# Two GLU steps earlier, in other buffers, and some additions from POOL to DVE

## The chip, the cores and the metric

The kernel runs on one core of a Trainium2 chip. The metric is the device time of one execution in microseconds (us), as the median of several runs. Engines are named as in the profile: PE multiplies matrices (PEld is its loading of weights), DVE, ACT and POOL work elementwise, SP issues transfers.

## What is computed

One layer of a streaming encoder over 2048 tokens of width 1024, all in float32.

```
hn = rmsnorm(h);  u, g_ssm, q, k, v, g_attn = split(hn @ W_in)
y_ssm = GLU(GELU(S5(u)))  * silu(g_ssm)     # zz = z @ w_glu + b;  val * sigmoid(gate)
y_att = stick_breaking(q, k, v, 8 heads x 64) * silu(g_attn)
h = h + concat(y_ssm, y_att) @ W_out
out = h + sigmoid(rmsnorm(h) @ W_pg) * (p @ W_pp)
```

Stick-breaking attention is swept in 128-query blocks over all earlier keys: a sigmoid of the scores, a reversed running product along the keys, and a product with the values.

## The kernel before

float32 products are made of three matmuls each (a high and a low part of both sides: hi·hi, hi·lo, lo·hi). The program has four stages in time: the projection of `u` with the S5 preparation, the S5 batches, the attention, and the output products.

The attention is a loop over 40 steps `t`. The eight heads are four pairs `hp`; pair `hp` handles query block `i = t - 8*hp`, so two pairs are under way in most steps, in steps 30 and 31 pairs 2 (blocks 14 and 15) and 3 (blocks 6 and 7), and from step 32 on pair 3 alone. Two blocks ahead of its attention a block is projected (`attn_proj`: 48 matmuls into `ps_q` on two banks, three transposes into `ps_tq`). `attn_block` walks the keys in chunks of 512, last chunk first. One chunk is a *turn*: six matmuls into two score banks `ps_z` (one per head), a sigmoid on ACT (`px`, L816), the running product on DVE (a scan, L821, which also reads `ps_z`), transposes into `ps_wt` (L526), two copies on ACT (`ws`, L835), and matmuls with the values into `ps_o` (L843). In a block's first chunk POOL masks the diagonal (L819).

Which PSUM banks these take is set by the step: before `glu_at` scores have three banks (`z0`, `z1`, `tr`) and projections `acc` and `ssm`; from `glu_at` on scores have two banks and projections `acc` and `tr`, since the GLU takes `ssm` (gate half, `ps_g`) and `acc` (value half, `ps_v`).

`glu_at` is 32. From then on every step has two of the 16 GLU units. A unit reads a 512x512 tile of the GELU output (`glu_z` loads it as `zt` and splits it into `zr`, once for four units), makes 24 matmuls, a sigmoid on ACT (L696), a product on DVE (L76), a product with the loaded gate on POOL (L698), and a store. Its buffers `gsm` and `glus` have two copies each. Every step from 32 on also makes one set of `cross_sums`: four loads, four subtractions on POOL (L874 to L877) and four stores, which prepare weights for the output products (a Strassen-like scheme with seven products in place of eight).

Key and value tiles lie in numbered slots; slots 2, 5, 6 and 7 are in pool `kv2`. Slot 6 holds keys of pair 1 last, slots 2, 5 and 7 keys of pair 2, up to step 31. Pool `wx` holds the first four weight tiles of pair 2, which its projections read up to step 29. The GLU's pool opens at step 32, where `kv2` and `wx` were.

In the output stage `cross_products` runs for eight pairs of blocks in `mixed_pair` and eight in `gated_pair`: on POOL it makes four additions `sx` (L912) per pair, each then split for a product by ACT (`yr`, L513) and DVE (`yr`, L65). The gated pairs end with a product on DVE, an addition on POOL (L1026) and a store.

The order on each engine is not that of the source: `plan` collects what each instruction needs, and `arrange` sets one fixed order per engine from estimated durations. The engines then run through their rows in that order, each waiting where an operand is late.

Of the kernel before, what the change touches and what calls it, by code (L numbers as in the profile page):

```python
# [8 lines left out]
F32 = mybir.dt.float32  # L9
# [4 lines left out]
ALU = mybir.AluOpType  # L14
# [4 lines left out]
P = 128  # L19
SEQ = 2048  # L20
DM = 1024
NT = SEQ // P
# [4 lines left out]
L = 16  # L27
# [643 lines left out]
def glu_z(e, pool, tb):  # L671

    zf = e.z_d.rearrange("j (k p) c -> p k j c", p=P)
    zr = pool.tile([P, 2, 4, 512], F32R, tag="zr", name="zr", bufs=1)
    for k in range(4):
        n = NCH // 4
        zt = pool.tile([P, L, n], F32, tag="zt", name="zt", bufs=2)
        e.nc.sync.dma_start(zt, zf[:, k, :, tb * n:(tb + 1) * n])
        hi, lo = (zr[:, s, k].rearrange("p (c j) -> p c j", j=L) for s in range(2))
        split(e, hi, lo, zt.rearrange("p j c -> p c j"))  # L680
    return zr


def glu_unit(e, pool, w, zr, tb, m):
    nc = e.nc
    gt = pool.tile([P, 512], F32, tag="gsm", name="gsm", bufs=2)
    nc.sync.dma_start(gt, e.gs_d[tb][m * P:(m + 1) * P])
    pg = e.bank("ps_g2", "ssm")
    pv = e.bank("ps_v2", "acc")
    cs = slice(m * P, (m + 1) * P)  # L690
    for half, ps in ((1, pg), (0, pv)):
        for c in range(4):
            wt = w[half][c]
            mm3(e, ps, (wt[:, 0, cs], wt[:, 1, cs]), (zr[:, 0, c], zr[:, 1, c]), c == 0, c == 3)
    sg = pool.tile([P, 512], F32, tag="glus", name="glus", bufs=2)
    nc.scalar.activation(sg, pg, AF.Sigmoid, bias=e.bglu[:, 4 + m:5 + m])  # L696
    stt(nc, sg, pv, e.bglu[:, m:m + 1], sg, ALU.add, ALU.mult)
    nc.gpsimd.tensor_tensor(sg, sg, gt, op=ALU.mult)  # L698
    nc.sync.dma_start(e.ys_d[tb][m * P:(m + 1) * P], sg)
# [158 lines left out]
    A.w += load_w(e, [cols[c, :, :, P * A.hp:P * (A.hp + 1)] for c in range(lo, hi)], 512, e.gmix, at=lo, **kw)  # L858


def cross_sums(e, pool, src, dst, scale, c):

    nc = e.nc
    t = []
    for i, j in ((0, 0), (0, 1), (1, 1), (1, 0)):
        a = pool.tile([P, 512], F32, tag="cs", name="cs", bufs=4)
        k = 4 * i + c
        nc.sync.dma_start(a, src[k * P:(k + 1) * P, 512 * j:512 * j + 512])
        if scale is not None:
            nc.scalar.activation(a, a, AF.Copy, scale=scale[:, k:k + 1])  # L870
        t.append(a)
    b11, b12, b22, b21 = t
    gp = nc.gpsimd.tensor_tensor
    gp(b11, b12, b11, op=ALU.subtract)  # L874
    gp(b12, b22, b12, op=ALU.subtract)
    gp(b22, b22, b11, op=ALU.subtract)
    gp(b21, b21, b22, op=ALU.subtract)  # L877
    for k, a in enumerate((b11, b22, b12, b21)):
        nc.sync.dma_start(dst[k][c * P:(c + 1) * P], a)
# [20 lines left out]
    return load_w(e, [d[c * P:(c + 1) * P] for c in range(4)], 512, None, **kw)  # L900


def cross_products(e, pool, name, q, w, early, late):

    nc = e.nc

    def f(tag, n):
        return pool.tile([P, 512], F32, tag=tag, name=tag, bufs=n)

    def add(a, b, op=ALU.add):  # L910
        t = f("sx", 3)
        nc.gpsimd.tensor_tensor(t, a, b, op=op)  # L912
        return t

    def product(ps, a, k, first):
        y = pool.tile([P, 2, 4, P], F32R, tag="yr", name="yr", bufs=4)
        split(e, y[:, 0].rearrange("p c t -> p (c t)"), y[:, 1].rearrange("p c t -> p (c t)"), a)
        for c in range(4):
            mm3x(e, ps, (y[:, 0, c], y[:, 1, c]), (w[k][c][:, 0], w[k][c][:, 1]), first and c == 0, c == 3, not first)

    ps = [e.bank(name, "z0", "z1", "acc", "ssm", "w0", "w1") for _ in range(4)]
    product(ps[0], q[0], 0, True)
    s1 = add(q[2], q[3])
    s2 = add(s1, q[0], ALU.subtract)
# [12 lines left out]
    late(3, None, None)  # L937
    s4 = add(q[1], s2, ALU.subtract)
    product(ps[2], s4, 5, False)
    late(1, ps[2], u)  # L940
    product(ps[3], q[3], 6, False)
    late(2, ps[3], u)


def mixed_pair(e, pool, far, j):

    nc = e.nc
    dma = (nc.sync if j else nc.gpsimd).dma_start
    q, h = [], []
    for k in range(4):  # L950
        i = 2 * j + k // 2
        y = pool.tile([P, 512], F32, tag="yq", name="yq", bufs=5)
        v = y.rearrange("p (c t) -> p c t", c=4)
        if k % 2:
            dma(v, e.ya_d[i].rearrange("c p t -> p c t"))
        else:
            dma(v, e.ys_d[i // 4][:, (i % 4) * P:(i % 4 + 1) * P].rearrange("(c p) t -> p c t", p=P))
        q.append(y)
    for k in range(4):
        i = 2 * j + k // 2  # L960
        x = far.tile([P, 512], F32, tag="h", name="h", bufs=7)
        dma(x, e.x[0, i * P:(i + 1) * P, 512 * (k % 2):512 * (k % 2) + 512])
        h.append(x)
    ss = pool.tile([P, 2, 2], F32, tag=f"ss{j}", name="ss")

    def early(u, ps, n):
        if n == 0:
            for k in (3, 1, 2):
                nc.gpsimd.tensor_tensor(h[k], h[k], u, op=ALU.add)
        vt(nc, h[3], ps, h[3], ALU.add)  # L970

    def late(k, ps, u):
        if ps is not None:
            vt(nc, h[k], ps, h[k], ALU.add)
        i, m = k // 2, k % 2
        jk = far.tile([P, 512], F32, tag="sg", name="jk", bufs=4)
        nc.scalar.activation(jk, h[k], AF.Square, accum_out=ss[:, i, m:m + 1])
        nc.sync.dma_start(e.h_d[2 * j + i][:, 512 * m:512 * m + 512], h[k])

    cross_products(e, pool, "ps_h", q, e.wo, early, late)  # L980
    r = pool.tile([P, 2], F32, tag=f"rs{j}", name="rs")
    vt(nc, r, ss[:, :, 0], ss[:, :, 1], ALU.add)
    vs(nc, r, r, 1.0 / DM, ALU.mult, EPS, ALU.add)
    nc.gpsimd.tensor_tensor(r, r, e.mhalf[:, :2], op=ALU.pow)
    return r


def gated_pair(e, pool, far, j, rs):

    nc = e.nc  # L990
    q, h = [], []
    for k in range(4):
        i, m = k // 2, k % 2
        t = far.tile([P, 512], F32, tag="h", name="h", bufs=7)
# [12 lines left out]
    o = [None] * 4  # L1007
# [6 lines left out]
    def late(k, ps, u):  # L1014
        i, m = k // 2, k % 2
        if o[k] is None:
            o[k] = far.tile([P, 512], F32, tag="sg", name="sg", bufs=4)
            if u is not None:
                vt(nc, o[k], ps, u, ALU.add)
        nc.scalar.activation(o[k], ps if k == 0 else o[k], AF.Sigmoid, scale=rs[:, i:i + 1])  # L1020
        pp = e.bank("ps_p", "tr", "o")
        ts = slice(i * P, i * P + P)
        for c in range(2):
            mm3x(e, pp, (pr[:, 0, c, ts], pr[:, 1, c, ts]), (e.wp[m][c][:, 0], e.wp[m][c][:, 1]), c == 0, c == 1)
        vt(nc, o[k], pp, o[k], ALU.mult)
        nc.gpsimd.tensor_tensor(o[k], o[k], h[k], op=ALU.add)  # L1026
        nc.sync.dma_start(e.out[0, (2 * j + i) * P:(2 * j + i + 1) * P, 512 * m:512 * m + 512], o[k])

    cross_products(e, pool, "ps_g", q, e.wg, early, late)
# [15 lines left out]
def hybrid_block_kernel(ctx: ExitStack, tc: tile.TileContext, x, xt, small, p, w_in, ssm_w_glu, w_out, w_ple_gate,  # L1045
                        w_ple_proj, out, rows, pools, dbg=None):
    nc = tc.nc
    e = Env()
# [118 lines left out]
    pk = pool(right, "pack", side="right")  # L1167
    early.close()
    e.stage = e.stage[:1]
    mid = ExitStack()  # L1170
    bp = pool(mid, "pb")
    with e.later():
        wgate = load_w(e, row_blocks(e.w_in[0], NC8, 512), 512, e.gmix)
# [39 lines left out]
    kv1 = pool(far, "kv1", side="right")  # L1213
    ap = pool(far, "attn", side="right")
    steps = NT + SKEW * (NHP - 1)
    glu_at = steps - 8
    for t in range(steps):
        e.z_banks, e.q_banks, e.o_banks = BANKS[2 if t < SKEW - 2 else t >= glu_at]
        for hp in range(NHP):
            if 0 <= t - SKEW * hp < NT:  # L1220
                attn_block(e, ap, A[hp], t - SKEW * hp)
        if t == glu_at:
            left.close()
            gl = pool(left, "glu")
            sums = pool(left, "sums")
        for hp in range(NHP):
            i = t - SKEW * hp
            if 0 <= i + 2 < NT and i + 2 >= (AHEAD if hp == 0 else 0):
# [5 lines left out]
        if t == AHEAD - 1:  # L1234
            left.close()
            e.xp = pool(ctx, "xp")
            kv2 = pool(left, "kv2")
            wx = pool(left, "wx")
        if t == glu_at - 3:
            wglu = glu_load(e)  # L1240
        if t >= glu_at:
            u = 2 * (t - glu_at)
            if u % 4 == 0:
                zr = glu_z(e, gl, u // 4)
            for k in range(u, u + 2):
                glu_unit(e, gl, wglu, zr, k // 4, k % 4)
            c = t - glu_at
            cross_sums(e, sums, *((w_out[0], e.so_d, None) if c < 4 else (w_ple_gate[0], e.sg_d, e.gple)), c % 4)
        if t == steps - 3:
            e.wo = [cross_weights(e, e.w_out[0], e.so_d, None, p) for p in range(2)]  # L1250
            wo4 = cross_weights(e, e.w_out[0], e.so_d, None, 4, pool=Halves(e))
    left.close()
    fin = pool(left, "fin")
    e.stage.append(pool(left, "fstage", 2))
# [354 lines left out]
```

## Time and profile before

| | |
|---|---|
| median of 3 runs | 1506.82 us (1503.86 to 1508.2) |
| the profiled execution | 1506.3 us, span 1504.5 us |
| busy: PE, PEld | 1452.0 us (97%), 1223.9 us (81%) |
| busy: DVE, ACT, POOL | 1010.2 us (67%), 811.4 us (54%), 486.2 us (32%) |
| mean granted PE clock | 0.991 |

Times of the profile are counted from the start of the span. A share is busy time by span; a matmul row's busy time includes its overlap with the next, so PE at 97% does not tell how densely its work stands. In a row of the timeline the first number is the start, the second the time from the first start to the last end of the instructions merged in it; what stands in square brackets is the engine's idle time ahead of it and who ended it.

### The profile page before, as it was taken

What the parts mean: (1) busy time and instruction counts of PE and PEld (TensorE: products, weight loads), DVE (VectorE), ACT (ScalarE), POOL (GpSimd) and SP (SyncE); (2) the same over time, 40 slices, a digit from 0 to 9 for tenths busy, and PEclk for the clock granted to TensorE, in tenths of its full rate; (3) what the DMA queues carried; (4) which work ended last, traced back from release to release, by engine and by line L of the source; (5) the groups of instructions that cost most, each with busy time, mean ns of one, the idle gap of its engine ahead of it and who ended that gap; (6) DMA issues with size and microseconds to landing.
All of it is one profiled execution on the core that took longest, in us unless ns stands there. A gap on an engine that the chain in (4) does not pass through costs nothing.

```text
span 1504.5 us, 33553 instructions
## 1 busy us (share of the span) xinstructions
PE 1452.0 (97%) x13068; PEld 1223.9 (81%) x13068; DVE 1010.2 (67%) x1802; ACT 811.4 (54%) x1764; POOL 486.2 (32%) x524
## 2 busy tenths in 40 slices
PE   5999999999999999999999999999999999999998
PEld 5999989988888888887788877777777888777776
DVE  8943887976667876676766775547777557744544
ACT  5654545565556765566555665545654436533332
POOL 3221454422222112211112343432145555434433
PEclk9999999999999999999999989999999999999999
DMA  8877736644333423334233577653467446523221
GB/s 292 292 261 241 227 123 201 191 165 158 124 127 125 155 94 129 123 117 132 96 125 100 176 240 205 214 159 91 139 205 253 159 155 201 156 67 111 75 68 58
DMA packets 178909, 238.21 MB, mean 158 GB/s; under 512 B 65744, under 2 KB 121024, under 8 KB 167616
## 3 DMA queue, kind: packets, MB, share of 16 engines
q1 hardware_dynamic: 176368, 227.49, 47.1%
q0 software_dynamic: 2384, 8.59, 2.0%
q8 instruction: 103, 1.69, 0.5%
q14 instruction: 54, 0.44, 0.1%
HBM read 166.94 MB, written 64.90 MB: 154 GB/s over the span
## 4 chain that ended last, share of the span: by engine, by line
PE 75%; DVE 10%; issue 5%; DMA 4%; ACT 3%; POOL 1%; SPq 1%; POOLq 0%; DVEq 0%; ACTq 0%
PE ps_q L745 20%; PE ps_o L843 7%; PE ps_z L812 6%; PE ps_wt L526 4%; PE ps_h L709 3%; PE ps_h L707 3%; PE ps_h L708 3%; PE ps_g L707 3%; PE ps_g L709 3%; PE ps_g L708 3%; DMA wst<-in_ssm_w_glu_dram 1%; PE ps_u L541 1%; PE ps_u L543 1%; PE ps_u L542 1%; DVE px L821 1%
## 5 line engine op out<-in xcount | busy, mean ns | idle before, releaser
L821 DVE TENSOR_TENSOR_SCAN px<-px,ps_z 128x512 f32<-128x512 f32 (+3 forms) x320 | 338.9, 1085 | 105.4 <-ACT px L816 60.5
L745 PE MATMUL ps_q<-w_w,xt 64*128 64x512 f32 x2784 | 375.0, 399 | 2.4 <-DVE glus L76 1.6
L745 PEld LDWEIGHTS ps_q<-w_w,xt 64*128 64x128 f32 x2784 | 269.6, 186 | 43.0 <-DVE glus L76 1.7
L816 ACT ACTIVATE px<-ps_z 128x512 f32<-128x512 f32 (+3 forms) x320 | 159.2, 534 | 77.7 <-PE ps_z L812 76.1
L835 ACT ACTIVATE ws<-ps_wt 128x512 f32<-128x512 f32 (+3 forms) x320 | 160.2, 537 | 73.0 <-PE ps_wt L526 72.0
L812 PE MATMUL ps_z<-k,q 64*128 64x512 f32 (+3 forms) x960 | 143.2, 387 | 7.3 <-DVE px L821 6.2
L843 PE MATMUL ps_o<-ws,v 128*64 128x128 f32 x2176 | 137.7, 279 | 0.3 <-ACT ws L835 0.2
L843 PEld LDWEIGHTS ps_o<-ws,v 128*64 128x64 f32 x2176 | 119.4, 139 | 18.4 <-issue 14.1
L507 POOL TENSOR_TENSOR rs_qk<-rs_qk,mhalf 128x4 f32<-128x4 f32 x64 | 67.2, 1049 | 193.3 <-DVE rs_qk L72 193.1
L526 PEld LDWEIGHTS ps_wt<-ident,px 64*128 64x128 f32 x2176 | 96.9, 139 | 27.0 <-ACT ws L835 8.0
L812 PEld LDWEIGHTS ps_z<-k,q 64*128 64x128 f32 x960 | 88.8, 189 | 28.5 <-issue 8.7
L526 PE MATMUL ps_wt<-ident,px 64*128 64x64 f32 x2176 | 103.4, 225 | 4.4 <-ACT ws L835 3.8
L819 POOL TENSOR_SCALAR_AFFINE_SELECT px<-px 128x128 f32<-128x128 f32 x128 | 40.0, 324 | 166.4 <-ACT px L816 158.7
L756 POOL TENSOR_TENSOR v<-qn,v 128x128 f32<-128x128 f32 x64 | 31.0, 484 | 170.3 <-DMA v<-qn 148.0
L541 PE MATMUL ps_u<-xt,w_w 128*128 128x256 f32 x256 | 74.5, 293 | 8.2 <-ACT w_w L491 6.9
L1026 POOL TENSOR_TENSOR sg<-sg,h 128x512 f32<-128x512 f32 x32 | 44.3, 1395 | 114.6 <-DVE sg L65 105.4
L543 PE MATMUL ps_u<-xt,w_w 128*128 128x256 f32 x256 | 73.4, 293 | 2.7 <-DVE w_w L76 2.7
L542 PE MATMUL ps_u<-xt,w_w 128*128 128x256 f32 x256 | 74.0, 290 | 0.5 <-DVE xt L65 0.5
L65 DVE TENSOR_TENSOR yr<-sx,yr 128x512 fp32r<-128x512 f32 x64 | 48.4, 780 | 34.8 <-ACT yr L513 33.8
L513 ACT ACTIVATE yr<-sx 128x512 fp32r<-128x512 f32 x64 | 39.2, 629 | 54.6 <-POOL sx L912 21.3
L65 DVE TENSOR_TENSOR qn<-ps_q,part 128x512 f32<-128x512 f32 x54 | 36.8, 682 | 42.2 <-ACT part L751 39.3
L65 DVE TENSOR_TENSOR yr<-yq,yr 128x512 fp32r<-128x512 f32 x48 | 53.5, 1115 | 12.4 <-ACT yr L513 12.4
(434 smaller groups left out, 3467.7 us busy)
## 6 DMA issues: line engine op xcount, KB each, us to landing
xt<-hn SPq DMA_DIRECT2D x58, 1024.0 KB
hn<-xt SPq DMA_DIRECT2D x16, 1024.0 KB
h<-h SPq DMA_DIRECT2D x64, 256.0 KB
wst<-in_w_in_dram SPq DMA_DIRECT2D x48, 256.0 KB
xg<-hn SPq DMA_DIRECT2D x12, 1024.0 KB
out_dram<-sg SPq DMA_DIRECT2D x32, 256.0 KB
x<-in_x_dram SPq DMA_DIRECT2D x14, 512.0 KB
h<-in_x_dram SPq DMA_DIRECT2D x28, 256.0 KB
```

The source lines that it names most:

```text
L65: nc.vector.tensor_tensor(out, a, b, op=op)
L526: e.nc.tensor.transpose(ps[h][:, 64 * k:64 * k + 64], v[r], e.ident[r, r])
L541: mm(out, wh, xh, start=first, stop=False)
L707: mm(out, xh, wh, start=first, stop=False, skip_group_check=more)
L708: mm(out, xh, wl, start=False, stop=False, skip_group_check=more)
L709: mm(out, xl, wh, start=False, stop=last, skip_group_check=more)
L745: nc.tensor.matmul(o, xt[r, a, c], A.w[c][r, b], start=c + s == 0, stop=c == NC8 - 1 and s == 2)
L812: nc.tensor.matmul(z[:, :n], q[half[h], a], A.k[ch][half[h], b, :n], start=s == 0, stop=s == 2)
L816: nc.scalar.activation(px[:, :n], z[:, :n], AF.Sigmoid, scale=-(HD ** -0.5))
L821: nc.vector.tensor_tensor_scan(rv, rv, z[:, :n][:, ::-1], initial=1.0 if carry[h] is None else carry[h], op0=ALU.mult, op1=ALU.bypass)
L835: nc.scalar.activation(dst, ps, AF.Copy, bias=1.0, scale=-1.0)
L843: nc.tensor.matmul(po[half[h], :P], A.v[sb][:, h], w[:, h, b], start=sb == i, stop=sb == 0)
```

## The change

`glu_at` becomes 30. The units are spread by a list: two in each of steps 30 and 31, one in each of steps 32 to 35, two in each of steps 36 to 39. The bank choice above moves with `glu_at`, so scores have two banks in steps 30 and 31 too. `zr` and `zt` (three copies in place of two) go where `wx` was. A unit's loaded gate and its result share one tile in a dead key slot of `kv2`: slot 6 alone for the four units of steps 30 and 31, slots 6 and 7 in turn after that. `cross_sums` stay with steps 32 to 39, now in key slots 2 and 5, both taken by every set. In the first two mixed pairs the `sx` additions are made by DVE, and in the last gated pair the final addition too.

```diff
 def glu_z(...):
-        zt = pool.tile([P, L, n], F32, tag="zt", name="zt", bufs=2)
+        zt = pool.tile([P, L, n], F32, tag="zt", name="zt", bufs=3)
-def glu_unit(e, pool, w, zr, tb, m):
+def glu_unit(e, old, slots, w, zr, tb, m):
-    gt = pool.tile([P, 512], F32, tag="gsm", name="gsm", bufs=2)
+    both = old(slots[m % len(slots)])
+    gt, sg = both[:, 0], both[:, 1]
...
-    sg = pool.tile([P, 512], F32, tag="glus", name="glus", bufs=2)
-def cross_sums(e, pool, src, dst, scale, c):
+def cross_sums(e, old, src, dst, scale, c):
-        a = pool.tile([P, 512], F32, tag="cs", name="cs", bufs=4)
+    rows = [b[:, k] for b in (old(2), old(5)) for k in range(2)]
 def cross_products(..., eng=None):
-        nc.gpsimd.tensor_tensor(t, a, b, op=op)
+        (eng or nc.gpsimd).tensor_tensor(t, a, b, op=op)
 def mixed_pair(...):
-    cross_products(e, pool, "ps_h", q, e.wo, early, late)
+    cross_products(e, pool, "ps_h", q, e.wo, early, late, nc.vector if j < 2 else None)
 def gated_pair(...):
-        nc.gpsimd.tensor_tensor(o[k], o[k], h[k], op=ALU.add)
+        (nc.vector if j == NT // 2 - 1 else nc.gpsimd).tensor_tensor(o[k], o[k], h[k], op=ALU.add)
 # the step loop
-    glu_at = steps - 8
+    glu_units = [[0,1],[2,3],[4],[5],[6],[7],[8,9],[10,11],[12,13],[14,15]]
+    def old(slot):
+        return kv2.tile([P, 2, 512], F32, tag=f"k{slot}", name="old", bufs=1)
+    glu_at = steps - 10
         if t == glu_at:
-            left.close()
-            gl = pool(left, "glu")
-            sums = pool(left, "sums")
+            over.close()
+            gl = pool(over, "glu")
...
-        if t == glu_at - 3:
+        if t == glu_at - 1:
             wglu = glu_load(e)
         if t >= glu_at:
...
+            for k in glu_units[t - glu_at]:
+                if k % 4 == 0:
+                    zr = glu_z(e, gl, k // 4)
+                glu_unit(e, old, (6, 7) if t >= glu_at + 2 else (6,), wglu, zr, k // 4, k % 4)
+            c = t - glu_at - 2
+            if c >= 0:
+                cross_sums(e, old, ...)
```

The order of PE up to about 836 us is that of before. In steps 30 and 31 of before, PE's order has this stretch, in which only score matmuls, transposes and value matmuls of the two pairs follow each other:

```order
L843 MATMUL ps_o<-ws,v 64x128 x14
L812 MATMUL ps_z<-k,q 128x512 x6
L526 MATMUL ps_wt<-ident,px 128x64 x16
L812 MATMUL ps_z<-k,q 128x512 x6
L526 MATMUL ps_wt<-ident,px 128x64 x16
L812 MATMUL ps_z<-k,q 128x512 x6
L843 MATMUL ps_o<-ws,v 64x128 x16
L526 MATMUL ps_wt<-ident,px 128x64 x16
L812 MATMUL ps_z<-k,q 128x512 x6
L526 MATMUL ps_wt<-ident,px 128x64 x16
L843 MATMUL ps_o<-ws,v 64x128 x16
L812 MATMUL ps_z<-k,q 128x512 x6
```

The same steps on PE now (`ps_g` and `ps_v` are the two halves of a GLU unit; the number behind them tells the units apart):

```order
L843 MATMUL ps_o<-ws,v 64x128 x14
L526 MATMUL ps_wt<-ident,px 128x64 x16
L812 MATMUL ps_z<-k,q 128x512 x6
L543 MATMUL ps_v_14428<-zr,w_w 128x512
L541 MATMUL ps_v_14428<-zr,w_w 128x512
L542 MATMUL ps_v_14428<-zr,w_w 128x512
L543 MATMUL ps_v_14428<-zr,w_w 128x512
L541 MATMUL ps_g_14816<-zr,w_w 128x512
L526 MATMUL ps_wt<-ident,px 128x64 x12
L843 MATMUL ps_o<-ws,v 64x128 x16
L542 MATMUL ps_g_14816<-zr,w_w 128x512
L812 MATMUL ps_z<-k,q 128x512 x6
```

Between two groups of score matmuls there are now GLU matmuls, while the later steps have fewer of them.

On DVE, where the first mixed pair begins, before (`w_w` and `w_wc` are weights being split, `yr` the operands of the products):

```order
L65 TENSOR_TENSOR w_w<-wst,w_w 128x512 x2
L65 TENSOR_TENSOR yr<-yq,yr 128x512
L65 TENSOR_TENSOR yat<-ps_o,g 128x128
L65 TENSOR_TENSOR w_wc<-wst,w_wc 128x512
L65 TENSOR_TENSOR yr<-sx,yr 128x512 x3
L65 TENSOR_TENSOR yr<-yq,yr 128x512
```

The same place on DVE now:

```order
L65 TENSOR_TENSOR yr<-yq,yr 128x512
L821 SCALAR_TENSOR_TENSOR px<-px,ps_z 128x512 x2
L912 TENSOR_TENSOR sx<-yq 128x512
L912 TENSOR_TENSOR sx<-sx,yq 128x512
L912 TENSOR_TENSOR sx<-yq 128x512
L65 TENSOR_TENSOR w_w<-wst,w_w 128x512
L65 TENSOR_TENSOR yr<-sx,yr 128x512 x3
```

The three sums have come to DVE, ahead of the splits that read them.

More of the change, by code (lines that the diff above doesn't have):

```diff
@@ L858, in attn_w @@
     A.w += load_w(e, [cols[c, :, :, P * A.hp:P * (A.hp + 1)] for c in range(lo, hi)], 512, e.gmix, at=lo, **kw)
-def cross_sums(e, pool, src, dst, scale, c):
+def cross_sums(e, old, src, dst, scale, c):
     nc = e.nc
     t = []
-    for i, j in ((0, 0), (0, 1), (1, 1), (1, 0)):
-        a = pool.tile([P, 512], F32, tag="cs", name="cs", bufs=4)
+    rows = [b[:, k] for b in (old(2), old(5)) for k in range(2)]
+    for (i, j), a in zip(((0, 0), (0, 1), (1, 1), (1, 0)), rows):
         k = 4 * i + c
@@ L900, in cross_weights, with cross_products @@
     return load_w(e, [d[c * P:(c + 1) * P] for c in range(4)], 512, None, **kw)
-def cross_products(e, pool, name, q, w, early, late):
+def cross_products(e, pool, name, q, w, early, late, eng=None):
     nc = e.nc
@@ L1169, in hybrid_block_kernel @@
     e.stage = e.stage[:1]
-    mid = ExitStack()
+    mid, over = ExitStack(), ExitStack()
     bp = pool(mid, "pb")
@@ L1237, in hybrid_block_kernel @@
             kv2 = pool(left, "kv2")
-            wx = pool(left, "wx")
-        if t == glu_at - 3:
+            wx = pool(over, "wx")
+        if t == glu_at - 1:
             wglu = glu_load(e)
         if t >= glu_at:
[L1242 to L1248, printed above, removed]
+            for k in glu_units[t - glu_at]:
[4 more added lines that the diff above has]
+            if c >= 0:
+                cross_sums(e, old, *((w_out[0], e.so_d, None) if c < 4 else (w_ple_gate[0], e.sg_d, e.gple)), c % 4)
         if t == steps - 3:
@@ L1251, in hybrid_block_kernel @@
             wo4 = cross_weights(e, e.w_out[0], e.so_d, None, 4, pool=Halves(e))
+    over.close()
     left.close()
```

## The prediction

> **What bounds the kernel now.** I read the page first, then the busy times by stretch, then the waits and the timeline where PE stands idle. The page says what fills the time:
>
> ```profile
> span 1504.5 us, 33553 instructions
> PE 1452.0 (97%) x13068; PEld 1223.9 (81%) x13068; DVE 1010.2 (67%) x1802; ACT 811.4 (54%) x1764; POOL 486.2 (32%) x524
> ```
>
> PE is the bound; the change leaves its matmuls as they are, so it can win only idle time and time at a low clock. The stretches show where these lie (columns: busy us and instructions of each engine, granted clock, DMA share, GB/s):
>
> ```profile
> core 0: us, PE busy (x) PEld busy (x) DVE busy (x) ACT busy (x) POOL busy (x), PEclk, DMA share, GB/s
> 845.00:890.00 45.00, 43.97 (x578) 35.97 (x576) 35.01 (x51) 29.62 (x69) 18.49 (x23) 1.00 0.70 228
> 890.00:930.00 40.00, 34.41 (x376) 26.89 (x373) 27.22 (x34) 25.84 (x52) 16.73 (x19) 0.83 0.75 213
> 930.00:1110.00 180.00, 176.51 (x1535) 140.12 (x1534) 110.94 (x148) 99.82 (x197) 54.95 (x58) 1.00 0.54 155
> 1110.00:1160.00 50.00, 45.45 (x213) 34.99 (x213) 40.38 (x48) 24.18 (x50) 30.68 (x23) 1.00 0.78 253
> 1160.00:1500.00 340.00, 335.62 (x1485) 265.74 (x1483) 185.16 (x251) 140.69 (x255) 148.73 (x108) 1.00 0.38 119
> ```
>
> From 890 to 930 us, steps 30 and 31 and the GLU's start, PE is idle for 40 − 34.41 = 5.59 us and has a clock of 0.83. The next are 1110 to 1160 us, the first two mixed pairs, with 4.55 us idle, and the nine times longer GLU steps with 3.49 us. Finer, the clock goes like this:
>
> ```profile
> 689.90:693.30 3.40, 1.30 (x18) 0.80 (x16) 0.89 (x2) 1.55 (x4) 0.00 (x0) 1.00 0.26 102
> 693.50:697.00 3.50, 3.50 (x28) 2.79 (x26) 3.36 (x6) 2.56 (x9) 0.00 (x0) 0.51 0.50 149
> 891.50:894.94 3.44, 1.94 (x24) 1.47 (x20) 2.56 (x5) 1.34 (x5) 2.54 (x4) 1.00 0.93 248
> 894.94:905.18 10.24, 9.10 (x73) 7.01 (x69) 8.59 (x12) 5.23 (x10) 3.04 (x4) 0.50 0.67 224
> 912.00:915.42 3.42, 1.89 (x29) 1.61 (x31) 3.02 (x4) 2.28 (x7) 0.54 (x2) 1.00 1.10 199
> 915.42:918.83 3.41, 3.41 (x24) 2.65 (x22) 1.93 (x2) 2.80 (x5) 0.00 (x0) 0.50 0.96 320
> ```
>
> Three times a stretch of 3.4 us in which PE was busy for 38 to 56% is followed by half the clock. In steps 30 and 31 PE worked 9.10 + 3.41 = 12.51 us at half clock, so 6.26 us of full-clock work were lost there, with the idle time 11.85 us. The waits there go round in a ring, scores to sigmoid to scan to the next scores:
>
> ```profile
> DVE px L821 <- ACT px L816: 5.0, 5, 2.1
> PE ps_z L812 <- DVE px L821: 4.0, 4, 1.5
> ```
>
> **The change part by part.**
>
> *Steps 30 and 31.* How long is a turn of that ring, and how much can PE do meanwhile? With three score banks (first three rows) and with two (last three), from the timeline:
>
> ```profile
> 893.97 0.93 PE L812 MATMUL ps_z<-k,q 64*128 64x512 f32 x5 [1.50 <-DVE px L821]
> 896.94 1.65 PE L812 MATMUL ps_z<-k,q 64*128 64x512 f32 x5 [0.47 <-DVE px L821]
> 900.23 1.64 PE L812 MATMUL ps_z<-k,q 64*128 64x512 f32 x5 [0.62 <-DVE px L821]
> ...
> 1082.45 0.96 PE L812 MATMUL ps_z<-k,q 64*128 64x512 f32 x6
> 1084.08 2.45 DVE L821 TENSOR_TENSOR_SCAN px<-px,ps_z 128x512 f32<-128x512 f32 x2 [1.19 <-ACT px L816]
> 1087.02 0.96 PE L812 MATMUL ps_z<-k,q 64*128 64x512 f32 x6
> ```
>
> Three banks: 2.97 and 3.29 us, held up by scans (partly at half clock). Two banks: 1087.02 − 1082.45 = 4.57 us; its scans end at 1086.53, so it could hardly be under 4.1. PE's own prices are steps between starts in a dense stretch:
>
> ```profile
> 882.83 0.86 PE L812 MATMUL ps_z<-k,q 64*128 64x512 f32 x6
> 883.52 0.86 PE L745 MATMUL ps_q<-w_w,xt 64*128 64x512 f32 x6
> 884.22 0.54 PE L526 MATMUL ps_wt<-ident,px 64*128 64x64 f32 x12
> 884.56 0.94 PE L745 MATMUL ps_q<-w_w,xt 64*128 64x512 f32 x6
> 885.43 1.97 PE L843 MATMUL ps_o<-ws,v 128*64 128x128 f32 x32
> ...
> 930.19 0.39 PE L541 MATMUL ps_v<-zr,w_w 128*128 128x512 f32 x1
> 930.42 0.40 PE L542 MATMUL ps_v<-zr,w_w 128*128 128x512 f32 x1
> ```
>
> Scores 0.69 us; 16 transposes 0.34 × 16/12 = 0.45; 8 value matmuls 8 × 1.97/32 = 0.49; a turn 1.63 us. A projection: 8 × 0.70 = 5.6, with its transposes some 5.9. A GLU unit: 24 × 0.23 = 5.5. Blocks 14 and 15 have four turns each, 6 and 7 two: six turns a step. Before, a step had 6 × 1.63 + 5.9 = 15.7 us for PE against 6 × 3.29 = 19.7 us of turns: 4 us a step lack, 8 in the two, and the clock does the rest. Now two GLU units add 11.0, so 26.7 us a step, against 6 × 4.57 = 27.4 on two banks. The two balance: 54.8 − 53.4 = 1.4 us idle, and 2.3% of 53.4 = 1.2 as in the dense steps at 845 to 890 (1.03 us of 45). Of 11.85 us some 2.6 stay: **−9.2 us** (bounds: −10.6 with the 2.3% alone; 0 if turns and filler miss each other). That the clock then stays full is read from the rows: no 3.4 us with PE under 56%, no halving. PE's whole idle time in the three stretches ahead of the halvings is 2.1, 1.5 and 1.5 us. The Trainium skill, "TensorE: Matmul & The Clock Gate", section "HAM oscillation — how this bites in real kernels", has the clock halved by idle gaps of over about 3.4 us; by that rule these halvings had another cause, filling would not remove them, and the sum would be some 6 us higher. Here the trace does not agree with the page's threshold, and I go by the trace.
>
> *Steps 32 to 37* have four units fewer, 22 us of cover for the waits. Their own work is 176.51 − 22 = 154.5 us. Bounds: the rate of today (3.49 of 180, 1.9%) gives 3.0 us, the rate of 890 to 930 (14%) 25 us. A step of one block with three turns has 3 × 1.63 + 5.9 + 5.5 = 16.3 us for PE against 13.7 of turns; so the low rates are nearer, and I take 4%: 6.2 us, **+2.7 us** (−0.5 to +21.5).
>
> *Buffers.* The first four units share one slot: the next sigmoid waits until the store before it has landed. What is queued behind it on ACT is `px` and `ws`, so PE through the ring. Product on POOL and a transfer, from the groups at 930 to 1110 us and the timeline:
>
> ```profile
> L698 POOL TENSOR_TENSOR glus<-glus,gsm 128x512 f32<-128x512 f32 x16 | 22.0, 1372 | 54.8 <-DVE glus L76 40.2 <-issue 14.5
> 862.48 0.61 SPq L486 DMA_DIRECT2D wst<-in_ssm_w_glu_dram x1
> 870.57 0.63 ACT L513 ACTIVATE w_w<-wst 128x512 fp32r<-128x512 f32 x1 [0.73 <-DMA wst<-in_ssm_w_glu_dram]
> ```
>
> A 256 KB transfer under load took 8.1 us from issue to use. From a unit's last matmul to the next sigmoid that is 0.7 (DVE) + 1.4 + 8.1 = 10.2 us; units come every 13.4 us, the sigmoid 2.8 us (half a unit) before its unit's end, so it is wanted after 10.6. It just fits; the GLU's loads and the moved sums queue on SP too. I take **+1.0 us** (0 to +14: four handovers of 3.5 us). The gate weights, used by the first units, land as late as 870.57 above and are now issued a few rows sooner, while the first GLU rows stand at about 860 us in PE's order and need the last weight some 13 us later: in that sum. The cross sums leave 845 to 900 us and come later, four POOL operations for a set as before; POOL is busy for 55 of 180 us there, which covers them.
>
> *Mixed pairs 0 and 1.* Eight `sx` sums go from POOL to DVE. The groups at 1110 to 1160 us, the waits of PE there, and one split alone:
>
> ```profile
> L912 POOL TENSOR_TENSOR sx<-yq 128x512 f32<-128x512 f32 x6 | 8.8, 1470 | 10.4 <-DMA yq<-ya 10.4
> L65 DVE TENSOR_TENSOR yr<-yq,yr 128x512 fp32r<-128x512 f32 x7 | 10.8, 1541 | 0.0
> PE ps_h L709 <- DVE yr L65: 2.6, 3, 1.6
> PE ps_h L707 <- ACT yr L513: 1.9, 1, 1.9
> 1110.28 0.68 DVE L65 TENSOR_TENSOR yr<-yq,yr 128x512 fp32r<-128x512 f32 x1
> ```
>
> A sum on DVE should take 0.68 us like that split, its like in shape and operands, against 1.47. Two in series stand before the operand for which PE waited 1.9 us: 2 × 0.79 = **−1.6 us**. Beside POOL's sums the splits take 1.54 in place of 0.68, so eight fewer sums give DVE back much of the 8 × 0.68 = 5.4 us that it takes on. Bounds: −4.5 (all idle time of PE there), +5.4 (all of it behind DVE, 81% busy).
>
> *The end.* The last rows of POOL and DVE:
>
> ```profile
> 1498.88 2.48 POOL L1026 TENSOR_TENSOR sg<-sg,h 128x512 f32<-128x512 f32 x2 [4.75 <-DVE sg L65]
> 1499.17 0.69 DVE L65 TENSOR_TENSOR sg<-ps_p,sg 128x512 f32<-128x512 f32 x1 [0.37 <-PE ps_p L709]
> ```
>
> POOL ends at 1501.36; on DVE the addition would follow at 1499.86 and end at 1500.54: **−0.8 us** (0 if DVE's earlier additions push the last product back).
>
> Sum: −9.2 + 2.7 + 1.0 − 1.6 − 0.8 = −7.9 us on the profiled execution's 1506.3, so 1498.4. The median of the runs lies 0.5 above that execution; against it I predict 1499.
>
> **The rivals.**
>
> *The clock stays halved* for its 12.5 us, for a cause other than the thin stretches. Then 6.3 us of the gain are missing: 1505. For it: no idle time over 2.1 us before any of the halvings. Against: all three come right behind a thin stretch. The clock gate's page of the Trainium skill, as read above, speaks for this rival.
>
> *Cover taken from the later steps is missing there*: 10% of 154.5 us idle, 15.5 in place of 6.2: 1508. For it: turns on two banks at 4.57 us leave a step of three turns only 2.6 us of spare work, and the fixed order must put it in the right places. Against: at 1082 us turns on two banks run with PE dense.
>
> *The one slot holds ACT*: if a store lands later than 8.5 us after its product, the sigmoid stands in ACT's queue and the ring with it. SP's queue can do that, since `ys` stores stand behind loads for the cross sums, which wait for keys of pair 2. At 3.5 us for each of four handovers it costs 14 in place of 1: 1512, slower.
>
> *It doesn't do what it says*: the weights come so late that PE stops at the first GLU rows; the order puts them behind the splits by 13 us, so I give this no chance of its own.
>
> **How the numbers follow.** Forecast 70%, clock 8%, later steps 10%, slot 12%. A measurement of this kernel can tell about 0.3%, 4.5 us, from no change. The forecast is faster by more, the two middle rivals are within it, the slot is slower: 0.70, 0.18, 0.12. Range: low, all favourable bounds, −10.6 − 0.5 + 0 − 4.5 − 0.8 = −16.4, 1489.9 on the profiled execution, taken as 1489; high, the later-steps rival with its 1508, rounded to 1509; only the slot's 12% lies outside.
>
> **What would show it.** Right: PE busy by over 95% and a clock of 1.00 where steps 30 and 31 stand, with GLU rows between the scores; turns of about 4.5 us; `sx` on DVE near 0.7 us, PE's 1.9 us wait for `yr` gone; the last addition ending 0.7 us behind the last product. Wrong: a clock of 0.5 in these steps (first rival); PE idle for over 10 us between the GLU's fifth unit and the first mixed pair (second); ACT idle ahead of the sigmoid L696 behind a store (third).

## The result, and the profile after

The changed kernel takes 1492.51 us (median of four runs, 1490.92 to 1495.42), the kernel before 1505.79 us (four runs, 1503.86 to 1508.2): 13.3 us less. The ratio is 0.9915, with a 95% interval from 0.9895 to 0.9934, so the gain is beyond the 0.3% that a measurement can tell. The profiled execution of the changed kernel took 1490.92 us, the fastest of its four, so the traces differ by 15.3 us where the medians differ by 13.3.

The page of the changed kernel: its span, and busy time, share and instructions of each engine.

```profile
span 1489.2 us, 33570 instructions
PE 1444.9 (97%) x13068; PEld 1220.6 (82%) x13068; DVE 1012.0 (68%) x1814; ACT 812.1 (55%) x1764; POOL 469.2 (32%) x512
```

PE makes the same 13068 matmuls with 7.1 us less busy time, in part because it spends less time at half clock. Where the time went is read from four landmarks on PE, which stand at the same place in its work in both traces: a group of score matmuls up to which PE's orders are alike, the first matmul of the first mixed pair, the 169th of the 672 on `ps_h` (each mixed pair makes 84, so two pairs are done; the orders differ a little there, hence L708 and L709), and the last matmul of all. From the timelines, before and then after:

```profile
832.98 0.94 PE L812 MATMUL ps_z<-k,q 64*128 64x512 f32 x6
...
1109.77 0.50 PE L707 MATMUL ps_h<-w_w,yr 128*128 128x512 f32 x1
...
1157.07 0.40 PE L708 MATMUL ps_h<-w_wc,yr 128*128 128x512 f32 x1
...
1498.67 0.39 PE L709 MATMUL ps_p<-w_wp,pr 128*128 128x512 f32 x1
```

```profile
831.45 0.94 PE L812 MATMUL ps_z<-k,q 64*128 64x512 f32 x6
...
1100.36 0.50 PE L707 MATMUL ps_h<-w_w,yr 128*128 128x512 f32 x1
...
1142.63 0.40 PE L709 MATMUL ps_h<-w_wc,yr 128*128 128x512 f32 x1
...
1484.05 0.39 PE L709 MATMUL ps_p<-w_wp,pr 128*128 128x512 f32 x1
```

At the first landmark the changed kernel is already 1.5 us ahead, though both have run the same order up to there: this part of the 15.3 us is not the change's. From there to the mixed pairs 7.9 us are gained (276.79 us before, 268.91 now), in the first two mixed pairs 5.0 more (47.30 before, 42.27 now), to the last matmul 0.2 more, and behind it 0.7 (the span ends 5.8 us after it before, 5.1 now): 13.8 us in all. The stretches of the changed kernel, with the columns of the prediction's view (busy us and instructions of each engine, granted clock, DMA share, GB/s):

```profile
845.00:890.00 45.00, 40.89 (x438) 32.44 (x436) 33.39 (x50) 26.99 (x60) 6.90 (x11) 0.96 0.56 141
890.00:930.00 40.00, 40.00 (x432) 31.68 (x431) 24.31 (x29) 22.48 (x44) 16.03 (x18) 1.00 0.53 177
930.00:1110.00 180.00, 176.04 (x1670) 139.90 (x1667) 124.91 (x167) 110.32 (x221) 70.42 (x74) 1.00 0.66 198
1100.00:1150.00 50.00, 49.64 (x246) 39.39 (x243) 39.77 (x60) 27.05 (x55) 18.87 (x17) 1.00 0.84 267
```

From 890 to 930 us, where PE had been idle for 5.59 us and at 0.83 of its clock, it is now busy for 40.00 of 40 at full clock. The stretch ahead of it, 845 to 890, has got worse: 4.11 us idle in place of 1.03, and a clock of 0.96. The timeline there shows a new wait:

```profile
861.68 0.63 ACT L513 ACTIVATE w_w<-wst 128x512 fp32r<-128x512 f32 x1 [4.26 <-DMA wst<-in_ssm_w_glu_dram]
862.22 0.58 ACT L751 ACTIVATE part<-ps_q 128x512 f32<-128x512 f32 x1
...
862.83 0.69 DVE L65 TENSOR_TENSOR qn<-ps_q,part 128x512 f32<-128x512 f32 x1 [4.78 <-ACT part L751]
...
863.58 0.79 PE L541 MATMUL ps_g<-zr,w_w 128*128 128x512 f32 x1 [3.19 <-DVE qn L65]
```

ACT stands for 4.26 us at the last tile of GLU weights. Behind it in ACT's queue is `part`, the copy that empties a projection's bank; DVE's `qn` waits for that, and PE's first GLU matmul for `qn`. PE does not wait for the weight as an operand alone: the load has turned into a wait of everything that stands behind it on ACT.

### The profile page after: what moved, and what is told of

It is laid out like the page before. It is cut to its first block, busy times and chain, and to the rows that moved or that the text cites. A ratio compares the mean times of both kernels' runs of the same rounds, so it can differ in the third digit from the quotient of the medians.

```text
span 1489.2 us, 33570 instructions
## 1 busy us (share of the span) xinstructions
PE 1444.9 (97%) x13068; PEld 1220.6 (82%) x13068; DVE 1012.0 (68%) x1814; ACT 812.1 (55%) x1764; POOL 469.2 (32%) x512
## 4 chain that ended last, share of the span: by engine, by line
PE 77%; DVE 9%; DMA 4%; issue 4%; ACT 3%; POOL 2%; SPq 1%; DVEq 0%; POOLq 0%; ACTq 0%
PE ps_q L745 20%; PE ps_o L843 7%; PE ps_z L812 6%; PE ps_wt L526 4%; PE ps_g L707 4%; PE ps_g L709 4%; PE ps_g L708 3%; PE ps_h L709 3%; PE ps_h L707 3%; PE ps_h L708 3%; DMA wst<-in_ssm_w_glu_dram 2%; PE ps_u L541 1%; PE ps_u L543 1%; PE ps_u L542 1%; PE ps_sg L541 1%
## 5 line engine op out<-in xcount | busy, mean ns | idle before, releaser
L812 PE MATMUL ps_z<-k,q 64*128 64x512 f32 (+3 forms) x960 | 138.0, 381 | 2.1 <-DVE px L821 1.1
L1026 POOL TENSOR_TENSOR sg<-sg,h 128x512 f32<-128x512 f32 x28 | 39.3, 1412 | 99.7 <-DVE sg L65 90.7
L541 PEld LDWEIGHTS ps_u<-xt,w_w 128*128 128x128 f32 x256 | 50.3, 197 | 8.9 <-ACT w_w L491 7.0
```

What stands on the lines that cost most here:

```text
L541: mm(out, wh, xh, start=first, stop=False)
L812: nc.tensor.matmul(z[:, :n], q[half[h], a], A.k[ch][half[h], b, :n], start=s == 0, stop=s == 2)
```

## Experiments

Each ratio is against the kernel before, with its 95% interval.

**1. The two parts apart.** The GLU part alone:

```
-    cross_products(e, pool, "ps_h", q, e.wo, early, late, nc.vector if j < 2 else None)
+    cross_products(e, pool, "ps_h", q, e.wo, early, late)
-        (nc.vector if j == NT // 2 - 1 else nc.gpsimd).tensor_tensor(o[k], o[k], h[k], op=ALU.add)
+        nc.gpsimd.tensor_tensor(o[k], o[k], h[k], op=ALU.add)
```

> The GLU part alone, all `sx` sums and final additions back on POOL. If the two parts are worth what the traces put on them (first mixed matmul 9.4 us sooner, then 4.0 and 1.0 in the first two mixed pairs and 0.7 at the end), it is 9.4 us faster than before: 1496.4 us, with PE waiting about 2 us for `yr` in each of the first pairs. The rival is that the pairs gained from the GLU's earlier end, since the weights and inputs for them are ready by then: 13 to 15 us faster, 1491 to 1493, with the pairs dense though POOL makes the sums.

And the DVE part alone, the same lines put into the kernel before:

> The DVE part alone on the kernel before. If the parts are independent: 4.0 + 1.0 + 0.7 = 5.7 us faster, 1500.1 us, and the first mixed matmul at 1109.8 as before. If the pairs gained from the GLU's earlier end: 1.6 us from the sums by the prediction's estimate and 0.7 at the end, 1503.5 us, with PE still short of work for over 3 us in the first two pairs.

Measured: the GLU part alone 1497.54 us (0.995, 0.9933 to 0.9967), the DVE part alone 1500.26 us (0.9967, 0.9953 to 0.998). Gains of 0.50% and 0.33% make 0.83%, and both together have 0.85%: within these intervals they add. The stretches with the first two mixed pairs, the GLU part alone first, the DVE part alone second (before: 45.45 of 50):

```profile
1103.00:1153.00 50.00, 47.91 (x236) 37.24 (x233) 39.70 (x50) 25.45 (x53) 29.06 (x23) 0.97 0.79 253
```

```profile
1110.00:1160.00 50.00, 50.00 (x274) 40.43 (x271) 38.73 (x58) 26.25 (x54) 17.97 (x16) 1.00 0.81 259
```

With the sums on DVE, PE is never idle there, though the GLU ends as late as before. With the sums on POOL it still loses 2.09 us and some clock; its longest wait there is 1.8 us behind DVE's `h`, not the wait for `yr` that I had expected. The rival that the GLU's earlier end filled the pairs falls. By the landmarks the two pairs take 44.14 us in the DVE part alone, 3.2 less than before, and 46.41 in the GLU part alone, 4.1 more than with both. One caution holds for all that follows: each edit gives a new instruction order, and this alone moves things by a few us. In the GLU part alone the first mixed pair starts at 1103.5 us, 3.1 later than with both parts, though its attention is written alike.

**2. The sums of all pairs on DVE.** Edit: `nc.vector if j < 2 else None` becomes `nc.vector`.

> The changed kernel with the `sx` sums of all eight mixed pairs on DVE, not of the first two alone. If the gain in the first pairs is that PE no longer waits for operands that come through POOL: nothing here, within 1 us of 1492.5, since PE is busy for 25.00 of 25 us in pairs 2 to 5 of the changed kernel. If POOL's sums slow DVE everywhere and that sets the pace: 0.5 to 1 us for each of six pairs, about 1488.

1495.18 us (0.9922, 0.9906 to 0.9937), no difference from the changed kernel that can be told. From 1145 to 1265 us DVE works 84.42 us and POOL 32.77; in the changed kernel a like stretch had 72.04 and 62.16; PE is busy for all of it in both:

```profile
1145.00:1265.00 120.00, 120.00 (x521) 96.44 (x520) 84.42 (x128) 55.81 (x115) 32.77 (x24) 1.00 0.58 183
```

```profile
1142.00:1262.00 120.00, 120.00 (x523) 96.40 (x522) 72.04 (x104) 54.94 (x114) 62.16 (x47) 1.00 0.55 178
```

The sums are worth something only where PE waits for them, in the first two pairs.

**3. The gate half first.** In each unit the gate half is multiplied first, but `glu_load` loads the value half first:

```
-    return [load_w(e, [rows[4 * c:4 * c + 4, :, 512 * k:512 * k + 512] for c in range(4)], 512, None) for k in range(2)]
+    return [load_w(e, [rows[4 * c:4 * c + 4, :, 512 * k:512 * k + 512] for c in range(4)], 512, None) for k in (1, 0)][::-1]
```

> The changed kernel with the gate half of the GLU weights loaded ahead of the value half, so that the half that a unit uses first is there first. If ACT's stand of 4.26 us at the last gate weight is what makes PE wait 3.2 us at the first GLU matmul and halves the clock for the 3.4 us behind it: both go, 3.2 + 1.7 = 4.9 us faster than the changed kernel, about 1488 us, with a clock of 1.00 from 845 to 930 us. If the wait belongs to the ring of scores at the start of step 30 (PE idle somewhere there in any case): within 1 us of the changed kernel, 1492.5, with another wait in its place. If the halving has a cause of its own: 3.2 us faster, 1489.3, clock still halved once.

1485.43 us (0.9871, 0.9853 to 0.9889), the fastest kernel of all, 0.44% under the changed one. Its waits of ACT from 836 to 900 us (us in total, times, longest) have one row for weights, and the stretch from 845 to 890 us has full clock again:

```profile
ACT w_w L513 <- DMA wst<-in_ssm_w_glu_dram: 0.9, 1, 0.9
```

```profile
845.00:890.00 45.00, 44.03 (x504) 33.87 (x501) 35.46 (x55) 30.98 (x67) 9.90 (x14) 1.00 0.63 152
```

The same row of the changed kernel, and of the kernel before, where the last of these loads is issued later (862.48 us against 850.41) and ACT converts it later still (870.57 against 861.68):

```profile
ACT w_w L513 <- DMA wst<-in_ssm_w_glu_dram: 5.1, 2, 4.3
```

```profile
ACT w_w L513 <- DMA wst<-in_ssm_w_glu_dram: 2.9, 2, 2.1
```

The wait cost 4.8 us here by the stretches: 3.14 us less idle time, and a half-clock stretch of 3.33 us less, worth 1.67. But the last tile did not come sooner for being of the other half. Its issue, its conversion and the first GLU matmul, with the gate half first:

```profile
858.19 1.64 SPq L486 DMA_DIRECT2D wst<-in_ssm_w_glu_dram  x1
865.75 0.63 ACT L513 ACTIVATE w_w<-wst 128x512 fp32r<-128x512 f32 x1 [0.92 <-DMA wst<-in_ssm_w_glu_dram]
872.75 0.50 PE L541 MATMUL ps_g<-zr,w_w 128*128 128x512 f32 x1
```

In the changed kernel the issue stands at 850.41 us, the conversion at 861.68 and the matmul at 863.58, and the issue takes 5.08 us on SP:

```profile
850.41 5.08 SPq L486 DMA_DIRECT2D wst<-in_ssm_w_glu_dram  x1
```

All three rows stand later now. So what the edit changed is the order: ACT comes to the last tile 4.1 us later, close to when it has landed, and PE to the GLU 9.2 us later.

**4. The step at which the GLU begins.** The new buffers and the sums on DVE kept, the start put at step 32 or at 31 (what hangs on `glu_at`, the bank choice and the step of the weight load, moves with it), or one unit in place of two in steps 30 and 31:

```
-    glu_units = [[0,1],[2,3],[4],[5],[6],[7],[8,9],[10,11],[12,13],[14,15]]
+    glu_units = [[0,1],[2,3],[4,5],[6,7],[8,9],[10,11],[12,13],[14,15]]        # glu_at = steps - 8
+    glu_units = [[0,1],[2,3],[4],[5],[6,7],[8,9],[10,11],[12,13],[14,15]]      # glu_at = steps - 9
+    glu_units = [[0],[1],[2,3],[4],[5],[6,7],[8,9],[10,11],[12,13],[14,15]]    # glu_at = steps - 10
```

> The changed kernel with the move alone undone: the GLU begins at step 32 again, two units in each step, with the two key slots and the later weight load kept, and the sums on DVE. If the gain lies in filling steps 30 and 31: PE is thin there again, half clock returns behind stretches in which it is busy for under 57%, and 8 to 9 us come back: about 1500.5 us, as with the DVE part alone on the kernel before (1500.3). If the gain came from the other buffers, the third bank or the loads instead: below 1495. If the buffers cost something by themselves: above 1503.

> The changed kernel with the GLU's start at step 31: two units there, one in each of steps 32 and 33, two in each later one. If each filled step is worth the same: half of the move's gain, 4.5 us slower than the changed kernel, about 1497, with half clock in step 30 alone. If only the grants of half clock count and step 30 alone is too short to bring one: 1 to 2 us slower, 1494. If the later steps' thinner cover is what costs, it is faster than the changed kernel.

> The changed kernel with one unit in place of two in each of steps 30 and 31 (and two in 32, one in 33 and 34, two from 35 on). If the balance of the prediction holds (turns on two banks 27.4 us a step, PE's work with one unit 21.2): PE lacks 6 us in each of the two steps, half clock comes back, and the move's gain is gone: 1500 us or more. If the turns are shorter than 4.57 us wherever PE is not full, so that any filler does: within 2 us of the changed kernel, 1491 to 1495.

Start at 32: 1492.5 us (0.9919, 0.9903 to 0.9935). Start at 31: 1492.61 (0.991, 0.9898 to 0.9922). One unit each: 1496.13 (0.9939, 0.9927 to 0.9951). With the move of two steps undone nothing is lost. My theory of the move falls in its plain form; the reason stands in the timelines. The first load of the GLU's input and the first GLU matmul, of the kernel before and then of the start at 32, with the latter's stretch from 890 to 930 us:

```profile
909.67 0.43 SPq L678 DMA_DIRECT2D zt<-z  x1
...
921.97 0.50 PE L541 MATMUL ps_g<-zr,w_w 128*128 128x512 f32 x1
```

```profile
842.04 1.28 SPq L678 DMA_DIRECT2D zt<-z  x1
...
893.00 0.50 PE L541 MATMUL ps_g<-zr,w_w 128*128 128x512 f32 x1
```

```profile
890.00:930.00 40.00, 38.72 (x448) 30.79 (x446) 27.27 (x37) 22.96 (x52) 13.59 (x17) 1.00 0.52 175
```

Written at step 32, the GLU still runs from 893 us, among the scores of steps 30 and 31: its buffers are free, and the instruction order puts rows wherever their buffers and operands allow. Before, the GLU's pool lay where keys are read until step 31, so its first load came at 909.67. So PE is filled from 890 to 930 us here too, while the DVE part alone, with the start at 32 in the old buffers, has 33.38 us of 40 there and a clock of 0.87. One unit each is 3.6 us slower than two, though the start at 32 has none there by its list, so the balance of work and turns by the list is not what decides. Its ACT stands 4.7 us at a `zr` load (waits from 836 to 880 us), and half clock for 6.8 us follows:

```profile
ACT zr L513 <- DMA zt<-z: 4.7, 1, 4.7
```

**5. Gate half first at the other starts.** The edit of experiment 3 with the start at 32 and at 31.

> The same kernel (start at step 32, new buffers, 1492.5 us) with the gate half of the GLU weights loaded first. If the late weights hold ACT and with it the ring of scores here too (PE idle 4.3 us from 845 to 890 us and half clock once there): 4 us faster, 1488.5. If beginning two steps sooner is worth something once the weights are there: 3 us or more above the 1485.4 of the start at step 30 with the gate half first. If the step number is worth nothing: 1485.5.

> The start at step 31 (1492.6 us) with the gate half loaded first. If the step number is worth nothing and the late weights cost what they do at step 30: 1485.5 to 1487. If the start at 31 had escaped the late weights already (no half clock near 860 us there, first GLU matmul at 877.7): 1491 to 1492.6.

At 32: 1487.47 us (0.9887, 0.9872 to 0.9903), 5 us faster than its parent, and by these intervals not to be told from the 0.9871 of the start at 30. At 31: 1495.45 us (0.9937, 0.9922 to 0.9951), slower than its parent, a miss. The waits at 31 from 836 to 900 us, ACT's and then PE's:

```profile
ACT w_w L513 <- DMA wst<-in_ssm_w_glu_dram: 4.7, 1, 4.7
```

```profile
PE ps_tq L526 <- ACT ws L835: 4.4, 1, 4.4
```

Here ACT still stands, for longer than in its parent (3.8 us). ACT's wait for these weights is 5.1, 3.3 and 4.7 us in kernels of 1492.5, 1492.5 and 1495.5 us, and 0.9 and 1.6 us in the two of 1485.4 and 1487.5. So the half that is loaded first does not decide by itself. The two kernels with the short wait are the fastest, which speaks for ACT's standing queue as the cost, but the start at 31 breaks the row: 3.8 us of wait and 1492.6 us, without a loss of clock there. Each of these edits also gives a new order, and no run shortened the wait alone.

**6. Keeping the GLU out of steps 30 and 31.** Two edits of the start at 32 were meant to hold it back. The first swaps the unit slots, `(6, 7)` to `(7, 6)`; the second lays the first load for `zr` into slot 7:

```
+        if tb == 0 and k == 0:
+            zt = old(7)[:, 0].rearrange("p (j c) -> p j c", j=L)
...
```

> The kernel that begins the GLU at step 32 in the new buffers (1492.5 us), with the two unit slots taken in the order 7, 6 in place of 6, 7. Slot 7 holds keys of pair 2 up to step 31, so the first unit's sigmoid has nowhere to write until then and all later units stand behind it; `zr` is loaded as early as before. If the gain of the new buffers is that GLU rows run ahead of their step number, into steps 30 and 31 (first GLU matmul at 893 us in place of 922): only the first unit's 24 matmuls can still do so, and most of the 7.2 us between the DVE part alone (ratio 0.9967) and this kernel's parent (0.9919) go: 1497.5 to 1500. If the gain comes from the cross sums' new place or the GLU weights' later load: 1492.5.

> The start at step 32 in the new buffers (1492.5 us) once more, with one edit: the first of the four loads for the first `zr` goes into key slot 7, which holds keys of pair 2 until the end of step 31 (free at about 903 us), in place of a place of its own that is free from step 29. Slots of the units, cross sums and weights stay where they are. If the gain of the new buffers is that `zr` can be filled early (loads at 842 to 873 us in place of 910 to 919) so that GLU rows run in steps 30 and 31: the first GLU matmul goes back to about 920 us, half clock returns there, and the time to that of the DVE part alone, 1500 us. If it is the cross sums' place or the later weight load: 1492.5 us.

1492.65 us (0.9912, 0.9896 to 0.9927) and 1498.12 us (0.9951, 0.9935 to 0.9967). The first took nothing back, but it had not held the GLU either; the second came near the 1500 us, but not for the reason given. The first GLU matmul and the stretch from 890 to 930 us, of the first kernel and then of the second:

```profile
895.94 0.50 PE L541 MATMUL ps_g<-zr,w_w 128*128 128x512 f32 x1
```

```profile
890.00:930.00 40.00, 38.72 (x473) 31.76 (x470) 24.61 (x35) 23.21 (x52) 15.60 (x18) 1.00 0.56 187
```

```profile
905.80 0.51 PE L541 MATMUL ps_g<-zr,w_w 128*128 128x512 f32 x1
```

```profile
890.00:930.00 40.00, 37.66 (x438) 29.76 (x435) 31.76 (x42) 27.12 (x57) 17.16 (x20) 1.00 0.70 199
```

Slot 7 is free soon after 900 us, so both still start 16 us or more ahead of the kernel before, and PE keeps full clock there. In the second the time went elsewhere. Its order differs from about 130 us on; it has half clock near 340 us, and by PE's count of matmuls it comes to the first landmark 5.2 us later than the start at 32 (838.74 us against 833.58). From there to the mixed pairs, the part that the edit was meant to slow, it takes 264.55 us, less than the start at 32 (271.04) and the changed kernel (268.91); then the first two mixed pairs take 46.6 us in place of 42.0. So these two say that a start at 896 or 906 us is early enough to fill the thin steps, and the 1498.12 us say nothing against an early start. They do not say how much of the gain is the early `zr` and how much the cross sums' new place; a kernel with the new buffers and a GLU start at 920 us was not run.

**7. One slot for all units.** Edit: `(6, 7) if t >= glu_at + 2 else (6,)` becomes `(6,)`.

> The changed kernel with slot 6 alone for all 16 units, not only for the first four. If a unit's store lands in time (10.2 us from the last matmul to the next sigmoid against the 10.6 us between them, the prediction's estimate), the twelve other handovers cost nothing either where units come one in a step, and a little where they come two in a step: 0 to 2 us slower than the changed kernel, 1492.5 to 1494.5. If one slot holds ACT as the third rival had it, 3.5 us for each of some twelve handovers: 30 us or more slower, above 1520; if only where two units share a step, eight handovers, 1510 to 1520.

1498.93 us (0.9964, 0.9949 to 0.9979): 0.49% slower than the changed kernel, between the two expectations. Its waits of PE from 836 us to the first mixed pairs:

```profile
PE ps_wt L526 <- ACT ws L835: 3.5, 2, 3.0
PE ps_h L707 <- DVE px L821: 2.8, 1, 2.8
```

The last score matmul starts at 1102.5 us in place of 1095.3, and 3.4 us of half clock follow. This kernel is slower, but not by a sigmoid that blocks the ring at each handover: ACT's idle time ahead of L696 from 860 to 1110 us is 4.0 us here and 16.5 in the changed kernel. Whether the slot or only the new order makes the last scores late was not settled.

## Why the prediction was right, and where it was not

I forecast 1499 us (1489 to 1509) by a gain of 7.9 us; it was 13.3 by the medians, 15.3 in the traces, 13.8 of them behind the first landmark. The time lies inside the range, but the terms do not hold one by one: the first gained less than forecast, the two costs hardly showed and the mixed pairs gained three times their share, so that errors of both signs cancel in part. Step by step:

*Steps 30 and 31: −9.2 forecast.* That filled turns keep PE dense at full clock is shown: 40.00 of 40 us from 890 to 930. The balance that I worked out is not what the trace has, though. The turns were to take 4.57 us; three score groups of these steps start like this:

```profile
910.19 0.96 PE L812 MATMUL ps_z<-k,q 64*128 64x512 f32 x6
...
915.21 0.96 PE L812 MATMUL ps_z<-k,q 64*128 64x512 f32 x6
...
919.64 0.96 PE L812 MATMUL ps_z<-k,q 64*128 64x512 f32 x6
```

From 893.98 to 930.61 us seven such gaps are 4.43 to 6.08 us, 5.2 on average. As PE is never idle there, its own work sets this pace and not the ring. By the stretches from 845 to 930 us the loss fell from 1.03 + 5.59 + 6.26 = 12.9 us to 4.1 + 1.7 = 5.8, so 7.1 us. What lacks is ACT's wait for the weight. My fourth rival was right in its cause and wrong in its path: I asked whether the weight arrives before PE needs it, and gave it no chance; it is ACT that stands at it, with `part` behind. Experiment 3, in which that wait is short, has 4.8 us less loss in the traces; with that, this term would have been near −12. The step number, on which my sum of units and turns rested, was not the cause (experiment 4). The new buffers are: with the start at 32 and the sums on DVE in both, 1500.26 us in the old ones and 1492.5 in the new. Which of the new places does it stays open (experiment 6).

*Steps 32 to 37: +2.7, and buffers: +1.0 forecast.* Neither is seen. From 930 to 1110 us PE is idle for 3.96 of 180 us; 4% of 154.5, the 6.2 us of the prediction, was too high. (The prediction calls these 180 us nine times longer than the 50 of the mixed pairs; they are 3.6 times as long, and no term rests on it.) From the first landmark to the mixed pairs the three terms make −5.5 us, and −7.9 were measured. Idle time and half clock account for 6.6 of these; the other 1.3 lie inside PE's busy time, and no run says where. For the one slot, ACT's waits from 860 to 1110 us have this row:

```profile
ACT old L696 <- issue: 11.7, 6, 4.5
```

And PE's from 836 to 1100 us:

```profile
PE ps_wt L526 <- ACT ws L835: 3.2, 3, 1.5
PE ps_g L541 <- DVE qn L65: 3.2, 1, 3.2
```

ACT does stand ahead of the sigmoid, but the third rival is not in this row: "issue" names no store, and only two of the six waits, 0.73 and 1.22 us, stand before 930 us, where the units share one slot. The other 9.7 us come where slots 6 and 7 take turns. Little of it reaches PE, which waits for ACT's `ws` 3.2 us in all and for no store.

*Mixed pairs: −1.6 forecast, −5.0 in the traces.* The mechanism was right, the size was not. I counted two sums in series on the way to one operand. The DVE part alone shows what that left out: all of PE's idle time in the stretch goes, 4.55 us, the bound that I had set as the best case. Two things come together. The sums take 0.68 us, as forecast, and DVE's splits take less because POOL's sums no longer run beside them. The groups of `yr` splits (duration ns as least, median, most) in the first two mixed pairs, before and after:

```profile
L65 DVE TENSOR_TENSOR yr<-yq,yr x7: 678/1784/2312, 1110.3 to 1150.0; 128x512 fp32r<-128x512 f32 x7
```

```profile
L65 DVE TENSOR_TENSOR yr<-yq,yr x6: 678/680/1450, 1105.1 to 1136.7; 128x512 fp32r<-128x512 f32 x6
L912 DVE TENSOR_TENSOR sx<-yq x4: 670/678/683, 1099.1 to 1122.2; 128x512 f32<-128x512 f32 x4
```

Of the seven splits before, the two that no POOL instruction overlaps take 0.68 us, and the five that one overlaps 1.75 to 2.31. The median falls from 1784 to 680 ns. I had counted this against DVE's added load only; since PE waited for these very splits (2.6 us behind `yr` on DVE before, 0.4 now), it belonged on the path. The Trainium skill, "SBUF — State Buffer", section "Who interferes with whom", says that a DVE instruction with two SBUF inputs contends with a GpSimd instruction that reads SBUF. These rows agree with it.

*The end: −0.8 forecast, −0.7 in the traces.* The addition starts 0.04 us after the last product ends:

```profile
1484.60 0.69 DVE L65 TENSOR_TENSOR sg<-ps_p,sg 128x512 f32<-128x512 f32 x1 [0.79 <-ACT sg L1020]
1485.33 0.69 DVE L1026 TENSOR_TENSOR sg<-sg,h 128x512 f32<-128x512 f32 x1
```

*The clock rival* fell: both halvings of steps 30 and 31 went with the thin stretches, and the one that came new stands right behind a new stall. *The later-steps rival* fell with the 3.96 us above.

## What to carry to other kernels

Where an order is made from buffers and operands, the memory that a stage waits for decides when it starts, more than the place in which it is written: ask which last reader frees its buffers. A load that "arrives in time" for its user can still be late for the engine that converts it, with everything queued behind that conversion; look at what is behind it, not only at who uses it. Compare two traces first at a place up to which their orders are alike; what differs there is not the change. When an addition moves from POOL to DVE, count what POOL's absence gives back to DVE's other instructions on the path, not the addition alone.

## What the runs showed of the hardware

The granted clock changes on a grid of 3.413 us: in every trace here the changes lie whole multiples of that apart. In the fourteen profiled executions there are 26 grants of half clock between 100 and 1475 us, and each follows a grid stretch in which PE was busy for 0 to 61% of the time. At full clock no such stretch under 47% went without one; from 47 to 61% it went both ways. Half clock ended behind a grid stretch in which PE was busy for 93% or more, and went on behind one of 49 to 89%. The two fastest kernels, 1485.4 and 1487.5 us, have none of the 26. The changed kernel's stall and the half clock behind it, then a stretch of 50% in the start at 31 that kept full clock (columns as above):

```profile
860.08:863.49 3.41, 0.31 (x6) 0.07 (x2) 0.66 (x2) 1.81 (x4) 0.00 (x0) 1.00 0.52 101
863.49:866.91 3.42, 3.33 (x23) 2.47 (x25) 3.42 (x7) 3.10 (x7) 0.00 (x0) 0.50 0.99 304
```

```profile
862.79:866.20 3.41, 1.71 (x40) 1.47 (x34) 0.21 (x1) 1.56 (x5) 0.69 (x2) 1.00 0.54 101
866.20:869.61 3.41, 3.32 (x34) 2.57 (x32) 2.96 (x7) 3.20 (x8) 1.40 (x3) 1.00 0.97 309
```

So PE's 1.70 us of idle time in a grid stretch went without half clock here, while the 1.50 and 1.53 us of the prediction's two stretches in steps 30 and 31 were followed by it: near half, the runs do not tell which way it goes. The Trainium skill, "TensorE: Matmul & The Clock Gate", section "What's actually happening", has a free-running window of 3413 ns, and the grid agrees with it. Its rule of idle gaps does not fit the halvings of the prediction, whose idle time was in pieces; a share of about half of the window does.
